# Block-product order, a sixth lead slab, and the state-space preparation of a hybrid retention / S5 decoder

## The chip, the cores and the metric

The kernel runs on one core of a Trainium2 chip. The metric is the device time of one execution in microseconds; the median of three runs before the change is 2788.43 us (2788.19 to 2794.11). The engines that matter here are PE (TensorE, the matrix multiplier), DVE (VectorE), ACT (ScalarE), POOL (GpSimd) and SP (SyncE, which issues most loads). Each engine runs its own list of instructions in the order in which the program wrote them, and waits on semaphores of the others. Matrix products accumulate in the banks of PSUM, 128 x 512 float32 numbers each.

## The reference

One sequence of 1024 tokens, width 1024, two layers: a retention mixer, then a state-space (S5) mixer. Each mixer is followed by a conv-gated MLP of inner width 2816, each sub-layer is normalised and shifted by a condition vector, and a final norm follows. What the change touches is the MLP's first half, and the tables of the S5 layer that depend on parameters alone:

```python
def conv_ffn(h, w_up, conv_w, conv_b, w_down):
    val, gate = jnp.split(h @ w_up, 2, axis=-1)
    gate = lax.conv_general_dilated(gate, conv_w, ...) + conv_b   # depthwise, causal, width 3
    return (jax.nn.silu(gate) * val) @ w_down

# s5_mixer: powers of exp((lam_re + i*lam_im)*dt) per group and state, hence cos and sin of many angles
for i in range(2):
    ...
    x = x + g1 * (retention_mixer(h, ...) if i % 2 == 0 else s5_mixer(h, ...))
    h = rms_norm(x) * (1.0 + sc2) + sh2
    x = x + g2 * conv_ffn(h, ...)
```

## The kernel before, in words

**One pair.** The 2816 columns of gate and val are cut into 22 slabs of 128. One slab of both is a *pair*. Its 2 x 2 block product (two halves of the tokens, two halves of the width) is not made with eight block products but with seven, named A11, S2, S3, S1, A22, A12, S4, and sums on both sides. Each is 4 slices x 3 matmuls of 128 x 512, since float32 operands are split into a high and a low part (`mm3`, L765 to L767, three lines for the three terms). So a pair is 84 matmuls.

**Banks and readers.** A11 goes to bank b1; ACT copies it to `u`, and A12 is later added into b1. S2 goes to b2, and DVE adds it to `u`. S3 goes to b4; DVE reads it (`g1 = u + b4`, L1210, in the profile `E<-tu,bk`), and A22 is then added into the same b4, which DVE reads again (`E<-tu,bk` a second time). S1 goes to b3, is read by DVE (`E<-E,bk`), and S4 is added into b3. A22 therefore waits for the `g1` addition: A22 overwrites what `g1` still has to read. After A22 come the convolution (`conv_start` on ACT, `conv_mid` L1638 and L1639 on DVE four times, `conv_end` on ACT) and two products by DVE.

**What feeds it.** The weights arrive in quarters. POOL makes sums of quarters (L128, `sq`, `wr`), and every one of the seven weight operands is split into high (L334, ACT) and low (L335, DVE) parts, two DVE instructions ahead in the schedule. `W.get` names the operand a product wants, and the order of the splits follows the order of the products (`Q7`).

**Lead slabs.** The MLP starts while the second half of the tokens is still being normalised. `lead()` computes A11 and A12 of the first `LEADS` slabs (24 matmuls each), which need the first half alone, keeping the results in SBUF tiles `uv`; the first `LEADS` pairs then run the five products `Q5` (S2, S3, S1, A22, S4). Meanwhile `Norm.steps_s`, a generator moved on by `nrm.step`, makes the sums of normalised halves (tiles `ht`, `hl`, `hg`) and their high and low parts (`hs`): the high by ACT, the low by DVE or POOL.

**Background work.** During the first MLP the S5 tables are made by `s5_weights`, a generator that `bg(steps)` moves on after each product of a pair, and by two after the last one. A `yield True` ends a call of `bg` at once. One block of eight (`j`) has two halves; each does outer products on POOL (L128, `ar<-sp`), transposes through bank 6 (L1392), five DVE instructions on angles (L1396 twice, L1398, L798, L1400; the tile `sev`), two Sin on ACT (L1402, L1403), a second outer product on POOL (9 columns), and matmuls into bank 7 (L1414).

## Time and profile before

| | |
|---|---|
| median of three runs | 2788.43 us |
| profiled execution, its own time | 2790.11 us |
| span of the profile | 2788.3 us |
| PE busy | 2628.9 us (94%), 12777 instructions |
| DVE busy | 1763.3 us (63%) |
| POOL busy | 1055.6 us (38%) |
| ACT busy | 932.5 us (33%) |
| chain that ended last | PE 64%, DVE 18%, ACT 6%, issue 4%, DMA 4%, POOL 2% |

The first MLP's up-projection runs from about 917 to 1445 us of the span (lead products, pairs 0 to 4 with five products, pairs 5 to 21 with seven), the second one's from about 2069 to 2521 us. In the views, "busy" is the time in which an engine executed; "idle before" is the time it stood still ahead of an instruction, with what ended that. PEclk is the clock that was granted to PE as a share of 2.4 GHz; at 0.5 it is 1.2 GHz. The kernel's own line numbers stand in the rows.

### The profile page before, as it was taken

Reading aid. Unit: us, or ns where it says so; the run is one execution under the profiler, and the core shown is the slowest. Engines: PE = TensorE matmul, PEld = TensorE weight load, DVE = VectorE, ACT = ScalarE, POOL = GpSimd, SP = SyncE. Lnnn points to the kernel's source line nnn. Section 1 sums busy time; section 2 is a strip of 40 time slices with the busy share of each in tenths; the row PEclk is TensorE's granted clock in tenths of the full one; section 3 lists DMA queues with packets and bytes.
Section 4 is the critical chain, followed back from the end, with each engine's and each line's share of the span. In section 5 each row is a group of like instructions: output and inputs, shape, how many; then the busy total and the mean of one; then the engine's idle time right before and its main releaser. Section 6 shows DMA issues by size and latency. Waiting matters only on the chain.

```text
span 2788.3 us, 33464 instructions
## 1 busy us (share of the span) xinstructions
PE 2628.9 (94%) x12777; PEld 2199.2 (79%) x12777; DVE 1763.3 (63%) x2347; ACT 932.5 (33%) x1486; POOL 1055.6 (38%) x817
## 2 busy tenths in 40 slices
PE   6999999999999888999989999999998999999998
PEld 5798888888888676777777877888876788888887
DVE  8664664746765787777776654674248876666454
ACT  5332131221322634444433323322144444343112
POOL 5455676765101544655523333221124422310004
PEclk7999999999999999999999999999999999999999
DMA  7644344343532223333345433795221322225211
GB/s 241 169 129 137 121 135 145 117 158 94 168 115 69 91 93 106 119 108 119 113 176 183 137 127 129 248 301 184 75 83 61 106 83 84 83 86 207 101 53 61
DMA packets 319756, 356.59 MB, mean 128 GB/s; under 512 B 39372, under 2 KB 261100, under 8 KB 319596
## 3 DMA queue, kind: packets, MB, share of 16 engines
q1 hardware_dynamic: 278316, 276.17, 31.7%
q10 hardware_dynamic: 41280, 78.28, 7.6%
q8 instruction: 101, 1.65, 0.2%
q14 instruction: 59, 0.48, 0.1%
HBM read 266.64 MB, written 86.15 MB: 127 GB/s over the span
## 4 chain that ended last, share of the span: by engine, by line
PE 64%; DVE 18%; ACT 6%; issue 4%; DMA 4%; POOL 2%; SPq 0%; ACTq 0%; DVEq 0%; POOLq 0%
PE bk L765 20%; PE bk L767 19%; PE bk L766 19%; DVE t L1639 1%; DVE t L1638 1%; DVE whi L335 1%; DVE E L1210 1%; DVE wlo L335 1%; PE bk L1077 1%; PE bk L1075 1%; PE bk L1076 1%; DVE t L1210 1%; DVE sev L1396 1%; POOL ar L128 1%; DMA U<-u_d 1%
## 5 line engine op out<-in xcount | busy, mean ns | idle before, releaser
L765 PE MATMUL bk<-hs,whi 128*128 128x512 f32 x656 | 268.4, 409 | 44.7 <-DVE E L1210 41.2
L1473 DVE SCALAR_TENSOR_TENSOR x<-bk,mods,x 128x512 f32<-128x512 f32 x224 | 184.6, 832 | 192.5 <-PE bk L767 192.4
L766 PE MATMUL bk<-hs,whi 128*128 128x512 f32 x656 | 265.5, 405 | 6.4 <-DVE hs L657 4.3
L322 DVE TENSOR_TENSOR wlo<-wr,whi 128x1024 fp32r<-128x1024 f32 x126 | 179.7, 1430 | 138.4 <-ACT whi L321 138.4
L765 PE MATMUL bk<-hh,whi 128*128 128x512 f32 x640 | 255.7, 400 | 8.3 <-DVE x L1473 4.1
L767 PE MATMUL bk<-hs,wlo 128*128 128x512 f32 x656 | 260.2, 397 | 0.0
L766 PE MATMUL bk<-hl,whi 128*128 128x512 f32 x640 | 253.4, 396 | 3.0 <-POOL hl L128 1.7
L765 PE MATMUL bk<-hs,wlo 128*128 128x512 f32 x576 | 229.4, 398 | 26.0 <-DVE E L1210 26.0
L767 PE MATMUL bk<-hh,wlo 128*128 128x512 f32 x640 | 252.4, 394 | 0.2 <-DVE wlo L322 0.2
L767 PE MATMUL bk<-hs,whi 128*128 128x512 f32 x576 | 231.0, 401 | 0.0
L766 PE MATMUL bk<-hs,wlo 128*128 128x512 f32 x576 | 227.1, 394 | 0.0
L321 ACT ACTIVATE whi<-wr 128x1024 fp32r<-128x1024 f32 x126 | 131.5, 1056 | 284.6 <-PE bk L766 226.1
L765 PEld LDWEIGHTS bk<-hs,whi 128*128 128x128 f32 x656 | 128.7, 196 | 78.2 <-issue 28.1
L765 PE MATMUL bk<-fh,whi 128*128 128x512 f32 (+1 forms) x480 | 183.2, 382 | 5.3 <-ACT nat L2229 3.7
L767 PE MATMUL bk<-fh,wlo 128*128 128x512 f32 (+1 forms) x480 | 181.0, 377 | 0.0
L766 PE MATMUL bk<-fl,whi 128*128 128x512 f32 (+1 forms) x480 | 180.8, 377 | 0.0
L457 POOL TENSOR_TENSOR aacc<-aacc,ar 128x1024 f32<-128x1024 f32 x70 | 172.4, 2463 | 5.8
L128 POOL TENSOR_TENSOR nacc<-nacc,ar 128x512 f32<-128x512 f32 x36 | 46.6, 1294 | 322.1 <-ACT ar L575 321.9
L766 PEld LDWEIGHTS bk<-hs,whi 128*128 128x128 f32 x656 | 129.4, 197 | 34.8 <-DVE hs L657 5.0
L765 PEld LDWEIGHTS bk<-hs,wlo 128*128 128x128 f32 x576 | 110.2, 191 | 53.9 <-ACT wlo L334 12.5
L765 PEld LDWEIGHTS bk<-hh,whi 128*128 128x128 f32 x640 | 122.3, 191 | 35.4 <-ACT hh L611 4.5
L128 POOL TENSOR_TENSOR ar<-sp 128x512 f32<-128x512 f32 (+1 forms) x64 | 83.2, 1314 | 175.8 <-ACT sev L1402 81.8
(375 smaller groups left out, 6706.1 us busy)
## 6 DMA issues: line engine op xcount, KB each, us to landing
ar<-in_ada_w SPq DMA_DIRECT2D x80, 512.0 KB, 4.4
wr<-in_ffn_w_up SPq DMA_DIRECT2D x74, 512.0 KB, 3.8
wr<-in_ret_w_in SPq DMA_DIRECT2D x48, 512.0 KB, 3.8
ff_d<-t ACTq DMA_DIRECT2D x44, 512.0 KB, 2.8
wr<-in_ffn_w_down SPq DMA_DIRECT2D x44, 512.0 KB, 4.2
fr<-ff_d SPq DMA_DIRECT2D x44, 512.0 KB, 5.8
x_d<-x ACTq DMA_DIRECT2D x24, 512.0 KB, 3.1
x<-x_d SPq DMA_DIRECT2D x24, 512.0 KB, 7.2
```

Source lines behind the costliest of these rows:

```text
L128: GP.tensor_tensor(out=out, in0=in0, in1=in1, op=op)
L321: A.activation(out=hi, in_=r, func=AF.Copy)
L322: low = lambda: V.tensor_tensor(out=lo, in0=r, in1=f(hi), op=ALU.subtract)
L335: V.tensor_tensor(out=lo, in0=src, in1=f(hi), op=ALU.subtract)
L457: eng.tensor_tensor(out=acc, in0=acc, in1=raw, op=ALU.add)
L765: PE.matmul(bk, lhsT=lh, rhs=rh, start=first, stop=False, skip_group_check=skip)
L766: PE.matmul(bk, lhsT=lh, rhs=rl, start=False, stop=False, skip_group_check=skip)
L767: PE.matmul(bk, lhsT=ll, rhs=rh, start=False, stop=last, skip_group_check=skip)
L1075: PE.matmul(o, lhsT=hh, rhs=wh[:, k % 4, :], start=(k == 0), stop=False)
L1076: PE.matmul(o, lhsT=hh, rhs=wl[:, k % 4, :], start=False, stop=False)
L1210: V.tensor_tensor(out=o, in0=a, in1=b, op=op)
L1473: V.scalar_tensor_tensor(out=dst, in0=bk, scalar=g, in1=src, op0=ALU.mult, op1=ALU.add)
```

## The change

It has four parts.

1. `Q7` has A12 ahead of A22, so that there are two products (S1, A12) between S3 and A22 in bank b4. The multiplication by b1 stays behind `conv_end`. `next_(5)` moves with A12.
2. `LEADS` is 6. `lead()` handles three slabs, then three; the val results of the last three stay in their PSUM banks until their pair has used them (`vv += bks`), so that the last two copies by ACT (L1759) go, and the lead pairs 0 to 2 rotate over three banks (2, 3, 4).
3. In `steps_s` six of the subtractions that make a low part per MLP go from POOL to DVE: two for t1, two for t3, two for t4.
4. In `s5_weights` the rounded angle `kq` lies in the `sev` tile and no longer in `tb`; the transposed outer product is copied out in two pieces (384 and 128 columns) into free ends of `tb` and `ta`, with two DMAs; `outer(9)` comes right behind the transposes and no longer behind Sin; each step ends its call of `bg`, and a pair moves the generator on once after each of six products and not at all after the seventh (before: eight).

The diff:

```diff
-    LEADS = 5
+    LEADS = 6
-    Q7 = ("A11", "S2", "S3", "S1", "A22", "A12", "S4")
+    Q7 = ("A11", "S2", "S3", "S1", "A12", "A22", "S4")
...
+    def hard(n):
+        for _ in range(n):
+            yield True
...
-                    parts(t1, S.t1, pool=True)
+                    parts(t1, S.t1, pool=i % 2 == 0)
...
-                parts(low[i], S.t3, pool=i % 2 == 1, then=partial(S.lh.put, low[i]))
+                parts(low[i], S.t3, then=partial(S.lh.put, low[i]))
...
-                parts(t2[i], S.t4, pool=i % 2 == 1, then=gone)
+                parts(t2[i], S.t4, then=gone)
...
-        kq = tb[:, HW:T]
+        kq = ev0
...
-                yield True
-                yield True
-                yield True
+                yield from hard(3)
                 bk = bank(6)
                 for g in range(4):
                     PE.transpose(bk[:, g * P:(g + 1) * P], ta[:, g * P:(g + 1) * P], ident)
-                A.activation(out=ev0, in_=bk, func=AF.Copy)
-                A.dma_start(out=p1_d[j, :, cs4], in_=ev0)
+                A.activation(out=tb[:, 640:T], in_=bk[:, 0:384], func=AF.Copy)
+                A.activation(out=ta[:, 896:T], in_=bk[:, 384:HW], func=AF.Copy)
+                A.dma_start(out=p1_d[j, :, hf * HW:hf * HW + 384], in_=tb[:, 640:T])
+                A.dma_start(out=p1_d[j, :, hf * HW + 384:(hf + 1) * HW], in_=ta[:, 896:T])
+                outer(9, O_AR, O_AI, O_Q1, O_Q2, False)
                 for c_ in (TWO_PI_1, TWO_PI_2):
                     V.scalar_tensor_tensor(out=ev1, in0=kq, scalar=-c_, in1=ev1, op0=ALU.mult, op1=ALU.add)
-                yield
+                yield True
                 V.scalar_tensor_tensor(out=ev1, in0=kq, scalar=-TWO_PI_3, in1=ev1, op0=ALU.mult, op1=ALU.add)
                 clamp_angle(ev1)
                 V.scalar_tensor_tensor(out=kq, in0=ev1, scalar=-1.0, in1=ev1, op0=ALU.mult, op1=ALU.max)
-                yield
+                yield True
...
-                yield
-                outer(9, O_AR, O_AI, O_Q1, O_Q2, False)
-                yield True
-                yield True
                 yield True
...
-                bg(steps * (2 if i == 6 else 1))
+                bg(steps if i < 6 else 0)
...
+            if val0 is None:
+                product(b1, q("A12"), SB.b1[4:8], False)
+                next_(5)
+                after(5)
             product(b4, q("A22"), SB.t4, False)
...
-            if val0 is None:
-                product(b1, q("A12"), SB.b1[4:8], False)
-                next_(5)
             tt(ts[:, 0, :], ts[:, 0, :], b1 if val0 is None else val0, ALU.mult)
...
-            uu = [tu[:, 0, :], tu[:, 1, :], halves[2], halves[4], halves[6]]
-            vv = [halves[0], halves[1], halves[3], halves[5], halves[7]]
+            uu = [tu[:, 0, :], tu[:, 1, :]] + halves[3:7]
+            vv = halves[0:3]
...
-            ws = [W.get(("uv", l, 3)), W.get(("uv", l, 4), more=True)]
+            ws = [W.get(("uv", l, i), more=(i > 3)) for i in range(3, LEADS)]
...
-            for i, bk in enumerate(bks):
-                A.activation(out=vv[3 + i], in_=bk, func=AF.Copy)
-                free_bank(bk)
-            W.done(2)
+            vv += bks
+            W.done(3)
...
-            else:
+            elif ff != 3:
                 drop(keep.pop(0))
+            if ff > 2:
+                free_bank(vv[ff])
```

**The order, place 1.** DVE in the first MLP, from behind the convolution of pair 15 to the `g1` addition of pair 16. `tu` is `u`, `bk` a bank; `whi` and `wlo` are the splits; `sev` are the angle steps; `E<-tu,bk` at the end is `g1`. Before (its `g1` comes two rows later, behind one more split):

```order
L335 TENSOR_TENSOR wlo<-wr,wlo 128x512
L1210 TENSOR_TENSOR t_7742<-t_7742,bk 128x512
L1210 TENSOR_TENSOR tu<-tu,bk 128x512
L1210 TENSOR_TENSOR t_7742<-t_7742,tu 128x512
L335 TENSOR_TENSOR whi<-sq,whi 128x512
L335 TENSOR_TENSOR wlo<-wrx,wlo 128x512
L1396 SCALAR_TENSOR_TENSOR sev<-ar,sev 128x512 x2
L335 TENSOR_TENSOR whi<-sq,whi 128x512
L1398 SCALAR_TENSOR_TENSOR sev<-ar,sev 128x512
L798 TENSOR_SCALAR sev<-sev 128x512
L1400 SCALAR_TENSOR_TENSOR ar<-sev 128x512
L1210 TENSOR_TENSOR tu<-tu,bk 128x512
```

After:

```order
L1214 TENSOR_TENSOR t_7742<-t_7742,bk 128x512
L1214 TENSOR_TENSOR tu<-tu,bk 128x512
L1214 TENSOR_TENSOR t_7742<-t_7742,tu 128x512
L335 TENSOR_TENSOR whi<-sq,whi 128x512
L335 TENSOR_TENSOR wlo<-wr,wlo 128x512
L335 TENSOR_TENSOR whi<-sq,whi 128x512
L1214 TENSOR_TENSOR tu<-tu,bk 128x512
L335 TENSOR_TENSOR wlo<-wrx,wlo 128x512
L1401 SCALAR_TENSOR_TENSOR sev<-sev 128x512 x2
L1214 TENSOR_TENSOR E<-tu,bk 128x8x64
L335 TENSOR_TENSOR whi<-wr,whi 128x512
L1403 SCALAR_TENSOR_TENSOR sev<-sev 128x512
```

Between the convolution's end and `g1`, five splits and all five angle steps lay before; now it is four splits and the first two angle steps, and the other three follow `g1`.

**Place 2.** DVE in the second MLP, pair 0, from the addition of S2 to `u` up to `g1`. `ht<-hf,ht` makes the difference of halves t4, `hs<-ht,hs` its low part. Before:

```order
L1210 TENSOR_TENSOR tu<-tu,bk 128x512
L706 TENSOR_TENSOR ht<-hf,ht 128x512 x2
L657 TENSOR_TENSOR hs<-ht,hs 128x512
L706 TENSOR_TENSOR ht<-hf,ht 128x512 x2
L657 TENSOR_TENSOR hs<-ht,hs 128x512
L1210 TENSOR_TENSOR E<-tu,bk 128x8x64
```

After:

```order
L1214 TENSOR_TENSOR tu<-tu,bk 128x512
L710 TENSOR_TENSOR ht<-hf,ht 128x512 x2
L661 TENSOR_TENSOR hs<-ht,hs 128x512
L710 TENSOR_TENSOR ht<-hf,ht 128x512
L661 TENSOR_TENSOR hs<-ht,hs 128x512
L710 TENSOR_TENSOR ht<-hf,ht 128x512
L661 TENSOR_TENSOR hs<-ht,hs 128x512 x2
L1214 TENSOR_TENSOR E<-tu,bk 128x8x64
```

Two more `hs<-ht,hs` stand ahead of `g1`.

**Place 3.** POOL at the same time. `hs<-...` are low parts (`ar` t1, `hl` t3, `ht` t4, `hg` the fourth set), the rest sums of weight quarters. Before:

```order
L128 TENSOR_TENSOR hs<-ar,hs 128x512 x4
L128 TENSOR_TENSOR hs<-hl,hs 128x512 x2
L128 TENSOR_TENSOR aacc<-wr 128x512
L128 TENSOR_TENSOR aacc<-aacc,wra 128x512
L128 TENSOR_TENSOR wr<-wra,wr 128x512
L128 TENSOR_TENSOR wra<-wra,aacc 128x512
L128 TENSOR_TENSOR hs<-ht,hs 128x512 x2
L128 TENSOR_TENSOR hs<-hg,hs 128x512 x2
```

After:

```order
L128 TENSOR_TENSOR hs<-ar,hs 128x512 x2
L128 TENSOR_TENSOR aacc<-wr 128x512
L128 TENSOR_TENSOR aacc<-aacc,wr 128x512
L128 TENSOR_TENSOR wr<-wr 128x512
L128 TENSOR_TENSOR wr<-wr,aacc 128x512
L128 TENSOR_TENSOR aacc<-wra 128x512
L128 TENSOR_TENSOR aacc<-aacc,wr 128x512
L128 TENSOR_TENSOR wra<-wr,wra 128x512
L128 TENSOR_TENSOR wr<-wr,aacc 128x512
L128 TENSOR_TENSOR hs<-hg,hs 128x512 x2
```

Six `hs` are gone (two of `ar`, two of `hl`, two of `ht`), and the sums of weights follow earlier.

## Rows read from the trace of the kernel before

**Rows 1.** Work by stretch: length, busy (count) per engine, PEclk, DMA share, GB/s

```profile
1072.60:1105.70 33.10, 23.28 (x96) 18.19 (x95) 25.42 (x29) 12.99 (x24) 16.31 (x13) 0.85 0.30 97
1105.70:1423.80 318.10, 291.29 (x1261) 234.95 (x1260) 240.82 (x288) 141.79 (x243) 170.90 (x138) 0.96 0.35 114
...
2216.50:2502.10 285.60, 285.60 (x1261) 236.56 (x1260) 195.07 (x271) 118.02 (x213) 79.80 (x57) 1.00 0.26 85
```

**Rows 2.** PE's waits, whole run: line <- releaser: us, times, longest

```profile
PE bk L765 <- DVE E L1210: 67.2, 21, 9.8
...
PE bk L1414 <- POOL ar L128: 12.5, 6, 3.1
...
PE bk L765 <- ACT uv L1751: 2.4, 2, 1.2
```

**Rows 3.** PE's waits, 1105.7 to 1423.8 (first MLP, pairs 7 to 20)

```profile
PE bk L765 <- DVE E L1210: 22.8, 7, 5.1
```

**Rows 4.** PE's waits, 1072.6 to 1105.7 (first MLP, pair 6)

```profile
PE bk L765 <- DVE E L1210: 9.8, 1, 9.8
```

**Rows 5.** PE's waits, 2106.4 to 2216.5 (second MLP, pairs 0 to 5)

```profile
PE bk L765 <- DVE E L1210: 16.2, 5, 5.9
```

**Rows 6.** VectorE's waits, 1105.7 to 1423.8

```profile
DVE wlo L335 <- ACT wlo L334: 29.6, 19, 3.3
...
DVE E L1210 <- PE bk L767: 7.7, 8, 1.9
```

**Rows 7.** VectorE's groups, 1105.7 to 1423.8: busy us, mean ns, idle before

```profile
L1638 DVE SCALAR_TENSOR_TENSOR t<-E,prm,t 128x512 f32<-128x512 f32 x28 | 29.7, 1062 | 10.7 <-ACT E L1628 10.7
...
L1396 DVE SCALAR_TENSOR_TENSOR sev<-ar,sev 128x512 f32<-128x512 f32 x14 | 19.3, 1376 | 0.8 <-POOL ar L1386 0.5
```

**Rows 8.** The same view, second MLP, 2216.5 to 2502.1

```profile
L1638 DVE SCALAR_TENSOR_TENSOR t<-E,prm,t 128x512 f32<-128x512 f32 x30 | 22.5, 749 | 5.7 <-ACT E L1628 5.7
```

**Rows 9.** VectorE in time, from pair 19 to pair 20: start, us, instruction

```profile
1390.82 0.68 DVE L1210 TENSOR_TENSOR E<-tu,bk 128x512 f32<-128x512 f32 x1
...
1398.68 0.69 DVE L335 TENSOR_TENSOR wlo<-wr,wlo 128x512 fp32r<-128x512 f32 x1 [1.31 <-ACT wlo L334]
...
1399.89 3.11 DVE L1396 SCALAR_TENSOR_TENSOR sev<-ar,sev 128x512 f32<-128x512 f32 x2
...
1404.22 0.69 DVE L1400 SCALAR_TENSOR_TENSOR ar<-sev 128x512 f32<-128x512 f32 x1
...
1411.41 0.67 DVE L1210 TENSOR_TENSOR E<-tu,bk 128x512 f32<-128x512 f32 x1
```

**Rows 10.** VectorE in time, from pair 5 to pair 6

```profile
1070.52 0.67 DVE L1210 TENSOR_TENSOR E<-tu,bk 128x512 f32<-128x512 f32 x1
...
1081.14 3.40 DVE L1396 SCALAR_TENSOR_TENSOR sev<-ar,sev 128x512 f32<-128x512 f32 x2
...
1092.81 0.67 DVE L1210 TENSOR_TENSOR E<-tu,bk 128x512 f32<-128x512 f32 x1
```

**Rows 11.** PE in time around pair 6's wait (start, us, instruction)

```profile
1093.63 0.77 PE L765 MATMUL bk<-hs,whi 128*128 128x512 f32 x1 [9.82 <-DVE E L1210]
1094.19 0.63 PE L766 MATMUL bk<-hs,whi 128*128 128x512 f32 x1
```

**Rows 12.** VectorE in time, second MLP's pairs 0 and 1

```profile
2111.37 2.88 DVE L706 TENSOR_TENSOR ht<-hf,ht 128x512 f32<-128x512 f32 x2
2114.18 1.76 DVE L657 TENSOR_TENSOR hs<-ht,hs 128x512 fp32r<-128x512 f32 x1
2115.86 3.42 DVE L706 TENSOR_TENSOR ht<-hf,ht 128x512 f32<-128x512 f32 x2
...
2119.81 0.68 DVE L1210 TENSOR_TENSOR E<-tu,bk 128x512 f32<-128x512 f32 x1
...
2136.53 0.69 DVE L1210 TENSOR_TENSOR t<-t,uv 128x512 f32<-128x512 f32 x1 [0.79 <-ACT t L1642]
```

**Rows 13.** What POOL waits for, whole run

```profile
POOL ar L128 <- ACT sev L1402: 81.8, 16, 12.2
```

More of the change, by code (lines that the diff above doesn't have):

```diff
@@ L1432, in s5_weights @@
                              in_=ks_d[j * 8:(j + 1) * 8, :, P - GI * t:2 * P - GI * t].rearrange("g i w -> i g w"))
-            yield True
-            yield True
-            yield True
-            yield True
-            yield True
-            yield True
+            yield from hard(6)
             A.activation(out=tb.rearrange("p (g j t) -> p g t j", g=8, t=8),
@@ L1441, in s5_weights @@
             A.dma_start(out=t_d[j], in_=tb)
-            yield True
-            yield True
+            yield from hard(2)
         drop(sev)
@@ L1702, in pair @@
                 free_bank(b1)
-                after(5)
             product(b3, q("S4"), SB.b2, False)
@@ L1751, in lead @@
                         A.activation(out=uu[3 + i], in_=bk, func=AF.Copy)
-                    if kh and i == 0:
+                    if kh and i == 1:
                         if not nrm.marked:
```

## The prediction, made before the changed kernel ran

> **What bounds the kernel now.** I read the work by stretch first, then what PE waits for, then VectorE's own waits, then VectorE in time at three places. PE is busy for 94% of the span, so a gain must be time in which PE stands still or runs at the lower of its two clocks. The second MLP's steady stretch shows what an undisturbed pair costs: 285.60 us for 15 pairs of 84 matmuls, PE busy throughout, clock 1.00 [rows 1]. So a pair is 285.60/15 = 19.04 us, a product 2.72 us, a matmul 0.2267 us. The first MLP's pairs 7 to 20 take 318.10 us at a clock of 0.96, although 14 undisturbed pairs are 266.6 us. Part of the rest is the state-space matmuls, the rest is waiting and clock.
>
> PE's largest wait, 67.2 us in 21 places, is for VectorE's addition into E (L1210) [rows 2]: a second product into bank b4 (A22) waits until `g1` has read S3's. Pairs 7 to 20 hold 22.8 us of it in 7 waits [rows 3], pair 6 alone 9.8 us in one [rows 4], the second MLP's lead pairs 16.2 us [rows 5]. Is VectorE late because it waits for PE, or because it has too much to do? In pairs 7 to 20 it waits ahead of an E addition for PE only 7.7 us in all, and 29.6 us for ACT's high halves of weights [rows 6]. So it is VectorE's own list that is late. Part of its length is stretching: a convolution step takes 1062 ns there [rows 7] against 749 ns in the second MLP [rows 8], where no state-space work runs beside it. An angle step takes 1376 ns [rows 7].
>
> The loop to look at runs from VectorE's second E addition of one pair (after A22) to `g1` of the next and to that pair's A22. PE does six products in it, 6 x 2.72 = 16.3 us. At pair 20 VectorE needs from 1390.82 to 1411.41 + 0.67, that is 21.3 us [rows 9]; the excess is PE's wait. A12 ahead of A22 by itself leaves this loop at six products; what it moves is how VectorE's work is shared. It puts 5.4 us of PE work behind S3, not 2.7 us, so that `g1` may come 2.7 us later, and the loop's next stretch loses as much.
>
> **The change part by part.** All sums are against the profiled execution of 2790.11 us; the median is 1.68 us lower, and I subtract that at the end.
>
> First MLP, pairs 7 to 20. With the new order one split of a weight leaves the stretch between the convolution and `g1`. At pair 20 that split is 0.69 us, with a wait of 1.31 us ahead of it [rows 9]. The convolution's end has to wait for the silu in its place, which costs about 0.8 us by the 0.79 us of idle time that a lead pair, without such a split, shows there [rows 12]; net 1.2 us for each of the 7 waits, 8.4 us. Second, the angle steps: counted in the two orders, 32 of the 45 that fall into the pairs lie in this loop's stretch from E to `g1` before, and 25 after, the others between `g1` and the second E, where PE now has three products (8.2 us) to hide them and had two. Five of them at pair 20 take from 1399.89 to 1404.91, 5.0 us or 1.0 us each [rows 9]. Of the 7 moved, 7/9 are in this stretch (7 of 9 half-blocks): 5.4 us. Together 13.8 of the 22.8 us; bounds 0 (VectorE is as late as before) and 22.8.
>
> With the waits some of the clock comes back: after pair 6's wait the next matmul stands with 0.63 us [rows 11], and 0.96 of 318.1 us leaves 12.7 us lost in the stretch [rows 1]. I take 5 us, a bit less than the share of the waits that goes (bounds 0 and 12.7).
>
> First MLP, pairs 0 to 6. The sixth lead slab gives PE 24 matmuls, 5.4 us, while VectorE still normalises: its lateness at pair 0 shrinks by as much. Pair 6's wait: from E at 1070.52 to `g1` at 1092.81 VectorE does all five angle steps, the first two in 3.40 us [rows 10]. In the new order the steps stand just behind `g1` of pair 6. I take 8 of the 9.8 us and 2.5 us of clock (0.85 over 33.1 us lost 5.0 [rows 1]). Against that: the steps before them now lie ahead of `g1` of pair 5, and pair 5 now has five products; 5 us by pair 20's steps, from 0 to 7. The lead pairs rotate over three banks, so S1 of a pair waits until VectorE has read S4's sum of the pair before: 2 us, from 0 to 5 x 0.68 = 3.4, if VectorE is on time. The moved subtractions: VectorE gets six in each MLP, POOL loses them. A subtraction took 0.68 to 1.76 us, and a difference of halves beside POOL 2.88/2 to 3.42/2 us [rows 12]. Two of the six stand ahead of pair 0's `g1`; the other four fall into the lead products' time, where the extra 5.4 us cover 4 x 0.68. So 1.4 us, from -3 (POOL no longer stretches the differences to 1.7 us) to 10.6 (six at 1.76, uncovered). Net for this stretch: -5.4 - 8 - 2.5 + 5 + 2 + 1.4 = -7.5.
>
> POOL's waits. The second outer product no longer stands behind the Sin, for which POOL waits 81.8 us in 16 places [rows 13]. PE's matmuls L1414 wait for that product 12.5 us in 6 places [rows 2]. I take 10 us (bounds 0 and 12.5). The extra copy and DMA on ACT cost nothing I can see: ACT is busy for 141.79 of 318.10 us [rows 1]; uncovered, 9 of them at the 0.68 us of an addition of that size [rows 9] would be 6.
>
> Second MLP. The sixth slab gives 5.4 us against the 16.2 us of waits [rows 5], the banks take 2, and the subtractions about nothing, since VectorE's stretch from 2111.37 to 2119.81 is half stretching already [rows 12]: -3.4. Of the waits for ACT's last copies of val, 2.4 us [rows 2], half goes: -1.2.
>
> Sum: -13.8 - 5 - 7.5 - 10 - 3.4 - 1.2 = -40.9. 2790.1 - 40.9 = 2749.2, less 1.7: **2747.5 us**.
>
> **The rivals.** *All of these waits go* (chance 0.12). VectorE has slack enough: in the second MLP it is busy for 195.07 of 285.60 us and PE never waits [rows 1]. Then 67.2 + 12.5 us of waits and 12.7 us of clock in pairs 7 to 20 go, less 7 for pair 5 and the banks: -85.4, 2703 us. Against it: in the first MLP VectorE is busy for 240.82 of 318.10 us, and 67 us of the remaining 77 would have to be usable.
>
> *VectorE stays the bound* (0.18). Steps that leave one half of the loop make the other half late: then the first MLP gains only POOL's 10 us and the second its 4.6: 2790.1 - 14.6 - 1.7 = 2774 us. For it: VectorE waits for PE only 7.7 us [rows 6].
>
> *It does not do what it says* (0.09). POOL's waits turn into waits for E at the same pairs, and the lead slab is used up by pair 5 and the subtractions: 2788 us, within a few us.
>
> *Slower by collision* (0.16). The second outer product is now issued in the same breath as the angle steps, so POOL works in SBUF while VectorE makes all five of them. Before, POOL waited for Sin and worked later. Then each step goes to the 1.7 us that the slowest pair of them shows (3.40/2 [rows 10]): two of them from the mean of 1.376 [rows 7], three from 0.69 at best (the last at pair 20 [rows 9]), 0.65 + 3.0 = 3.65 us for each of 9 half-blocks, 32.9 us. Less the 14.6 above: +18.3, 2807 us. It decides once VectorE's list in a loop grows by more than what the new order takes from it (13.8 us in the 14 pairs); for it speaks that almost nothing on VectorE there waits for PE [rows 6].
>
> The convolution steps show the stretching: 1062 against 749 ns [rows 7, 8]. The Trainium skill, "SBUF — State Buffer", section "Who interferes with whom", says of it that VectorE and GpSimd share one pair of ports under an exclusive lock, so that a VectorE instruction which needs that second pair (two SBUF inputs) and a GpSimd instruction keep each other out. The trace agrees: the E additions, which take one input from PSUM, kept 0.67 to 0.68 us beside it [rows 9, 10]. By the rule alone the collision rival would be the likeliest, with 2807 us. I leave it at 0.16: of pair 20's five steps the first two took 3.11 us and the last 0.69 [rows 9], so a run of steps is not stretched throughout.
>
> **How the numbers follow.** The forecast has 0.45; its own range is 2725 to 2770, from the bounds of the terms taken together. A measurement of this kernel can tell about 0.2%, 5.6 us, from no change. Faster than that are the forecast, the full gain and VectorE as the bound: 0.45 + 0.12 + 0.18 = 0.75; the same 0.09; slower 0.16. The range leaves out the collision (0.16) and little else: from 2700, just under the full gain, to 2790, just over no change.
>
> **What would show each step.** Right: PE's wait for E (L1210) falls from 67.2 to 40 us or less, pair 6's 9.8 us wait is gone, L1414's waits fall below 4 us, the stretch of pairs 7 to 20 takes about 295 us at a clock of 0.97 or more, and a new small wait stands at S1 in lead pairs. Wrong: the waits for E keep their sum and stand elsewhere (VectorE is the bound); L1396's mean rises from 1376 to 1600 ns or more (collision); the lead pairs' waits rise, so the moved subtractions were dearer than the cover of the sixth slab.

## The result

The changed kernel takes 2818.24 us (median of four runs, 2816.87 to 2819.31); the kernel before, run beside it, 2790.06 us. The ratio is 1.0099, 95% interval 1.0081 to 1.0116: **1% slower, 28 us, where 41 us of gain were forecast**. The time lies above the stated range, 28 us beyond its upper end of 2790.

Work by stretch, the changed kernel (columns as in [rows 1]). The stretches are: first MLP's lead products, pairs 0 to 5, pair 6, pairs 7 to 20, pair 21 with the down projection; second MLP's lead products, pairs 0 to 5, pairs 6 to 20:

```profile
921.10:969.40 48.30, 40.16 (x160) 31.14 (x161) 36.69 (x45) 30.16 (x49) 22.71 (x17) 0.89 0.23 73
969.40:1078.40 109.00, 89.93 (x374) 71.76 (x373) 85.03 (x108) 42.12 (x78) 47.30 (x36) 0.92 0.29 91
1078.40:1101.90 23.50, 21.76 (x90) 17.18 (x89) 22.50 (x22) 8.64 (x17) 17.23 (x13) 0.93 0.26 79
1101.90:1427.60 325.70, 293.90 (x1270) 235.17 (x1269) 249.60 (x292) 146.72 (x258) 175.99 (x141) 0.95 0.35 114
1427.60:1735.60 308.00, 281.54 (x1242) 227.00 (x1241) 181.22 (x203) 100.55 (x129) 106.00 (x93) 0.97 0.43 147
2090.30:2141.60 51.30, 40.71 (x161) 31.65 (x160) 36.18 (x45) 28.97 (x48) 21.21 (x16) 0.90 0.17 52
2141.60:2247.70 106.10, 91.89 (x361) 73.65 (x360) 82.80 (x107) 40.41 (x75) 37.74 (x25) 0.90 0.25 80
2247.70:2533.30 285.60, 285.60 (x1261) 236.56 (x1260) 195.58 (x273) 117.26 (x212) 86.09 (x59) 1.00 0.28 89
```

The same view of the kernel before, for the stretches that do not stand in [rows 1]:

```profile
918.20:955.80 37.60, 33.09 (x136) 26.29 (x137) 28.32 (x42) 28.35 (x46) 18.28 (x16) 0.91 0.20 65
1423.80:1715.50 291.70, 278.77 (x1242) 226.13 (x1241) 171.58 (x200) 98.56 (x119) 97.18 (x92) 0.98 0.44 153
2067.00:2106.40 39.40, 33.44 (x137) 26.10 (x137) 27.98 (x42) 27.30 (x45) 17.01 (x15) 0.91 0.13 41
```

Lead products and pairs 0 to 6 of the first MLP gained: from 187.5 to 180.8 us (pair 6 from 33.1 to 23.5). Pairs 7 to 20 lost 7.6 us (318.1 to 325.7), the stretch of pair 21 and the down projection **16.3 us** (291.7 to 308.0, with the same 1242 matmuls), the second MLP's lead products and pairs 0 to 6 **7.9 us** (168.6 to 176.5; pair 6 is 19.04 in the changed kernel). The steady second MLP is 285.6 us in both.

What PE waits for over the whole run, changed kernel (answers to [rows 2]; L769 is the old L765, L1394 the old L1392, L1415 the old L1414):

```profile
PE bk L769 <- DVE E L1214: 36.1, 16, 7.5
...
PE bk L1394 <- POOL ar L128: 11.4, 4, 5.0
PE bk L769 <- DVE tu L1214: 10.7, 3, 5.1
...
PE bk L769 <- ACT sev L1407: 8.6, 1, 8.6
PE bk L769 <- DVE uv L1214: 7.6, 4, 2.4
...
PE bk L769 <- ACT tu L1659: 6.5, 3, 3.7
...
PE bk L1415 <- POOL ar L128: 1.8, 2, 1.2
```

Read it against [rows 2]: the wait for E fell from 67.2 to 36.1 us and the one at the state-space matmuls from 12.5 to 1.8, both as forecast. That is 41.8 us less. But four waits came up (10.7 + 8.6 + 7.6 + 6.5), and the transposes L1394 wait for POOL for 11.4 us (4.0 before): together 40.8 us more. Over the whole span PE stands still for 179.8 us (159.4 before), and its same 12777 instructions keep it busy for 7.6 us more.

### The profile page after: what moved, and what is told of

It reads as the page before. It is cut to its first block, busy times and chain, and to the rows that moved or that the text cites. A ratio compares the mean times of both kernels' runs of the same rounds, so it can differ in the third digit from the quotient of the medians.

```text
span 2816.3 us, 33497 instructions
## 1 busy us (share of the span) xinstructions
PE 2636.5 (94%) x12777; PEld 2201.5 (78%) x12777; DVE 1780.8 (63%) x2357; ACT 931.5 (33%) x1496; POOL 1051.4 (37%) x805
## 4 chain that ended last, share of the span: by engine, by line
PE 59%; DVE 16%; issue 8%; ACT 6%; POOL 5%; DMA 4%; SPq 1%; ACTq 1%; POOLq 0%; DVEq 0%
PE bk L769 18%; PE bk L771 18%; PE bk L770 18%; POOL ar L128 3%; DVE t L1634 2%; DVE t L1633 1%; DVE wlo L335 1%; DVE E L1214 1%; PE bk L1081 1%; PE bk L1079 1%; PE bk L1080 1%; DVE whi L335 1%; DVE hs L661 1%; DMA fr<-ff_d 1%; SPq L1432 1%
## 5 line engine op out<-in xcount | busy, mean ns | idle before, releaser
L769 PE MATMUL bk<-hs,whi 128*128 128x512 f32 x664 | 268.7, 405 | 33.9 <-DVE E L1214 13.0
L769 PE MATMUL bk<-hs,wlo 128*128 128x512 f32 x568 | 231.9, 408 | 44.4 <-DVE E L1214 23.2
L771 PE MATMUL bk<-hs,wlo 128*128 128x512 f32 x664 | 269.4, 406 | 2.4 <-DVE wlo L322 2.4
L769 PE MATMUL bk<-hh,whi 128*128 128x512 f32 x640 | 255.3, 399 | 9.4 <-DVE x L1468 5.9
L770 PE MATMUL bk<-hs,wlo 128*128 128x512 f32 x568 | 228.8, 403 | 0.0
L769 PE MATMUL bk<-fh,whi 128*128 128x512 f32 (+1 forms) x480 | 183.1, 381 | 3.7 <-ACT nat L2224 3.1
L769 PEld LDWEIGHTS bk<-hs,whi 128*128 128x128 f32 x664 | 128.9, 194 | 68.3 <-issue 13.9
L128 POOL TENSOR_TENSOR nacc<-nacc,ar 128x512 f32<-128x512 f32 x36 | 46.6, 1294 | 335.7 <-ACT ar L579 335.6
L769 PEld LDWEIGHTS bk<-hs,wlo 128*128 128x128 f32 x568 | 111.2, 196 | 74.6 <-DVE E L1214 22.1
L771 PEld LDWEIGHTS bk<-hs,wlo 128*128 128x128 f32 x664 | 131.2, 198 | 31.8 <-DVE wlo L322 3.3
L769 PEld LDWEIGHTS bk<-hh,whi 128*128 128x128 f32 x640 | 122.4, 191 | 36.3 <-ACT hh L615 6.3
```

The costliest lines, as they stand in the source:

```text
L128: GP.tensor_tensor(out=out, in0=in0, in1=in1, op=op)
L769: PE.matmul(bk, lhsT=lh, rhs=rh, start=first, stop=False, skip_group_check=skip)
L770: PE.matmul(bk, lhsT=lh, rhs=rl, start=False, stop=False, skip_group_check=skip)
L771: PE.matmul(bk, lhsT=ll, rhs=rh, start=False, stop=last, skip_group_check=skip)
```

## The experiments

Each kernel was timed beside the kernel before. The columns of this table are the medians' difference to that (us), the ratio's 95% interval, and from each profile four stretches: first MLP from its lead products to the end of pair 6; pairs 7 to 20; pair 21 and down projection; second MLP from its lead products to the end of pair 6.

| kernel | difference | ratio, interval | 0 to 6 | 7 to 20 | 21, down | second, 0 to 6 |
|---|---|---|---|---|---|---|
| before | | | 187.5 | 318.1 | 291.7 | 168.6 |
| changed | +28.2 | 1.0081 to 1.0116 | 180.8 | 325.7 | 308.0 | 176.5 |
| a_only | -4.8 | 0.9972 to 0.9994 | 179.7 | 313.6 | 294.2 | 167.0 |
| l_only | +15.1 | 1.0037 to 1.0073 | 189.2 | 317.6 | 297.6 | 175.1 |
| s_only | +29.2 | 1.0083 to 1.0126 | 192.6 | 331.7 | 304.8 | 168.3 |
| no_s | +10.4 | 1.0025 to 1.0046 | 187.2 | 312.9 | 299.9 | 173.9 |
| p_only | +2.6 | 0.9999 to 1.0021 | 186.9 | 318.9 | 292.2 | 172.3 |
| s_gap | +37.5 | 1.0124 to 1.0154 | 182.5 | 320.5 | 328.6 | 170.2 |
| s_fix | -3.6 | 0.9979 to 0.9998 | 188.4 | 318.6 | 285.7 | 169.0 |
| b3 | +2.7 | 1.0001 to 1.0022 | 186.4 | 317.8 | 290.1 | 173.0 |
| l4 | +12.3 | 1.0034 to 1.0064 | 189.5 | 317.4 | 298.0 | 176.0 |
| l_t4 | +14.4 | 1.0030 to 1.0069 | 188.8 | 317.7 | 297.4 | 176.0 |
| lead4 | +11.5 | 1.0028 to 1.0057 | 184.5 | 317.1 | 300.3 | 172.9 |
| a_sfix | -4.9 | 0.9976 to 0.9994 | 178.8 | 314.7 | 291.6 | 168.4 |
| l_sfix | -4.8 | 0.9972 to 0.9991 | 181.4 | 325.2 | 282.3 | 175.4 |
| after_sfix | **-11.9** | 0.9944 to 0.9974 | 176.4 | 317.4 | 286.5 | 172.9 |
| after_tb | +17.6 | 1.0053 to 1.0087 | 181.2 | 324.5 | 299.5 | 173.7 |
| aps_fix | -5.5 | 0.9966 to 0.9989 | 180.8 | 314.2 | 291.4 | 168.5 |

### The parts one by one

The diffs of a_only, l_only, s_only and p_only are the parts 1, 2, 4 and 3 of the change; no_s is parts 1 to 3.

> The kernel before with A12 ahead of A22 alone (Q7 and the place of the product and its step). Theory 1 (the order is a gain, as forecast: one split and some angle steps leave the loop): about 14 us faster, PE's wait for E at A22 falls from 67 us to about 50. Theory 2 (VectorE's list stays the bound, the loop is six products either way): 0 +- 5 us, and the waits for E keep their sum. Theory 3 (the order brings its own wait: A12 now follows A11's copy by three products, not four, and S4 follows A22's reader): 5 to 10 us slower, with PE waiting for ACT's copy of u at A12.

The order is a gain, smaller than theory 1 has it: 4.8 us, with the wait for E at 52.0 us (forecast about 50). It brings the wait of theory 3 too, but a short one: at pair 6 the 9.8 us of [rows 4] become 3.6 us, now at A12. PE's waits with the order alone, first in pair 6, then for E in pairs 7 to 20, where they were 22.8 us [rows 3]:

```profile
PE bk L765 <- ACT tu L1664: 3.6, 1, 3.6
...
PE bk L765 <- DVE E L1210: 14.1, 7, 3.6
```

> The kernel before with six lead slabs alone, three of them kept in PSUM, and the three-bank rotation that follows. Theory 1 (the extra slab covers VectorE, as forecast: 5.4 us in each MLP against 2 for the banks): 5 to 10 us faster. Theory 2 (the rotation over three banks makes S1 of each lead pair wait for VectorE's reading of S4's sum of the pair before, which stands late in VectorE's list; in the changed kernel these waits are 9.4 us in the first MLP and 9.8 us in the second): about 10 us slower over both MLPs, and most of the 7.9 us that the second MLP's lead stage grew by in the changed kernel shows here.

15 us slower, more than either theory says. The second MLP's share of it, 6.5 us, is there as theory 2 has it; how it comes about is tested below.

> The kernel before with the state-space part alone (angle buffer, early second outer product, even steps). Theory 1 (POOL's waits go, as forecast): about 10 us faster, waits at the matmuls L1414 fall from 12.5 us to about 2. Theory 2 (what the early outer product takes from one wait it gives to the next: the transposes wait for POOL instead, and in the down projection each step of the generator now ends its call, so the work falls on other places): about 16 us slower, nearly all of it between the first MLP's last pair and the end of its down projection, where the changed kernel lost 11 to 16 us.

Nearer to theory 2, but 13 us worse: the part alone costs as much as the whole change. And the loss is not where theory 2 puts it: more than half of it lies in the pairs (5.1 and 13.6 us), the rest in the down projection (13.1 us).

> The changed kernel without its state-space part (order, lead slabs and moved subtractions stay). If the state-space part makes the loss (theory 2 of that run): about 16 us faster than the changed kernel, so 10 to 13 us slower than before. If the loss is the lead slabs' banks and the order: still 25 to 28 us slower than before. If the parts only cost together: near the time of before.

The first of the three: 10.4 us slower than before, so 18 us of the 28 go with the state-space part.

> The moved subtractions alone (six in each MLP from POOL to VectorE). Forecast: about 1.4 us slower in the first MLP and nothing in the second. By the three parts measured so far (order -5, lead slabs +15, and +10 for these three together) it should be 0 +- 3 us. Rival (VectorE is the bound in the lead stage, so six more of its instructions at 0.68 to 1.76 us in each MLP show in full): 8 to 15 us slower.

Six more subtractions for VectorE in each MLP cost 2.6 us, which this cannot tell from nothing (the interval holds 1); the rival falls.

### What the state-space part does wrong

The last two half-blocks, in time. First the kernel before, PE's state-space matmuls and VectorE's first two angle steps (start, us, instruction, idle before and what ended it):

```profile
1621.25 0.89 PE L1392 MATMUL bk<-cst,ar 128*128 128x128 f32 x4 [3.33 <-POOL ar L128]
1632.58 1.05 PE L1414 MATMUL bk<-ar,sp 128*16 128x128 f32 x8 [0.86 <-POOL ar L128]
1639.82 0.60 PE L1392 MATMUL bk<-cst,ar 128*128 128x128 f32 x4
```

```profile
1624.63 2.43 DVE L1396 SCALAR_TENSOR_TENSOR sev<-ar,sev 128x512 f32<-128x512 f32 x2 [1.69 <-POOL ar L1386]
```

Then the changed kernel: PE, VectorE, ACT and POOL at that place.

```profile
1625.94 0.66 PE L1394 MATMUL bk<-cst,ar 128*128 128x128 f32 x4 [1.47 <-POOL ar L128]
1633.98 1.05 PE L1415 MATMUL bk<-ar,sp 128*16 128x128 f32 x8 [1.22 <-POOL ar L128]
1646.37 1.11 PE L1394 MATMUL bk<-cst,ar 128*128 128x128 f32 x4 [5.00 <-POOL ar L128]
```

```profile
1629.32 3.35 DVE L1401 SCALAR_TENSOR_TENSOR sev<-sev 128x512 f32<-128x512 f32 x2 [1.03 <-POOL sev L1390]
...
1633.25 1.22 DVE L1403 SCALAR_TENSOR_TENSOR sev<-sev 128x512 f32<-128x512 f32 x1
```

```profile
1635.70 0.72 ACT L1407 ACTIVATE sev<-sev,cst 128x512 f32<-128x512 f32 x1 [6.00 <-DVE sev L1405]
...
1638.60 1.19 ACT L1417 ACTIVATE sev<-ar 128x512 f32<-128x512 f32 x1 [1.56 <-DMA cs_d<-sev]
...
1640.19 0.38 ACT L1422 ACTIVATE ar<-bk 16x256 f32<-16x256 f32 x1 [0.40 <-ACT sev L1417]
```

```profile
1640.64 0.24 POOL L128 TENSOR_TENSOR ar<-ar,db 16x32 f32<-16x32 f32 x1 [6.72 <-ACT ar L1422]
...
1641.95 2.17 POOL L128 TENSOR_TENSOR ar<-sp 128x512 f32<-128x512 f32 x2
```

From the bottom up: the next transposes wait for POOL's outer product, which stands in POOL's list behind the small addition L128; that waits for ACT's copy L1422; that stands behind the permuted copy L1417, which waits for the stores of cos and sin; and all of it stands in ACT's list behind Sin, which waits 6.00 us for VectorE's last angle step. The early outer product has left this circle, but Sin has not: PE had the matmuls done at 1635, and their result is fetched at 1640. A round takes 20.4 us (1625.94 to 1646.37) where it took 18.6, and all of the difference lies ahead of Sin, which comes 9.8 us after the transposes (7.8 before, Sin at 1629.00); from Sin to the next transposes it is 10.7 us, and was 10.8. Two things make Sin late here. The first two angle steps, now beside POOL's early outer product, take 3.35 us (2.43 before) and the third 1.22 (0.69 before). And each step ends its call of `bg`, so that an addition of the down projection, 0.74 us, has come between the second step and the third.

So POOL's wait for Sin, 81.8 us in [rows 13], did not go. It stands some instructions later now, at ACT's copy, and with the wait that was already there the sum is nearly the same: 81.8 + 68.4 = 150.2 us before, 150.7 now. POOL's wait for this copy in the kernel before, and then in the changed kernel:

```profile
POOL ar L128 <- ACT ar L1421: 68.4, 29, 9.6
```

```profile
POOL ar L128 <- ACT ar L1422: 150.7, 31, 13.1
```

Three kernels test this.

s_gap: part 4 alone, and behind Sin's stores

```diff
-                yield True
+                yield from hard(3)
```

> The state-space part alone, with two more steps between Sin and the matmuls L1414 (three steps lie between them, as between the early outer product and the matmuls before). Theory (the loss of this part is that Sin, the stores of cos and sin, and the copy into the same tile now stand one step ahead of the matmuls' evacuation, so ACT waits for the stores, POOL for ACT and the next transposes for POOL): ACT's wait for the stores, 19.9 us in 10 places in the run of that part alone, falls below 5 us, POOL's 178 us of waiting for ACT's copy L1422 shrinks, and 15 us or more of the 29 us come back. Rival (the early outer product itself collides with the angle steps): the 29 us stay.

The wait for the stores falls to 4.4 us as expected, and against the part alone the pairs come back (10.1 us in 0 to 6, 11.2 in 7 to 20). Yet the kernel is slower, because the generator has more steps and is not through when the last group of the down projection begins: what is left is then issued at once (`bg_drain`). ACT waits there for a load of that work, and the split that PE needs stands behind it in ACT's list. PE's waits from pair 21 to the end of the down projection in s_gap:

```profile
PE bk L1394 <- POOL ar L128: 17.4, 4, 9.5
PE bk L769 <- ACT whi L321: 14.4, 1, 14.4
PE bk L1415 <- POOL ar L128: 10.7, 2, 5.9
```

s_fix: part 4 alone, matmuls and evacuation ahead of Sin, the permuted copy in `tb`

```diff
-                A.activation(out=ev0, in_=kq, func=AF.Sin, ...)   # and the second Sin, both stores
-                yield True
                 w9 = ta[:, 0:576].rearrange("p (g w) -> p g w", g=4)
...
-                A.activation(out=ev0.rearrange(...), in_=w9[...], func=AF.Copy)
-                A.dma_start(out=w1_d[j, :, cs4], in_=ev0)
+                A.activation(out=tb[:, 0:HW].rearrange(...), in_=w9[...], func=AF.Copy)
+                A.dma_start(out=w1_d[j, :, cs4], in_=tb[:, 0:HW])
...
+                yield True
+                A.activation(out=ev0, in_=kq, func=AF.Sin, ...)   # and the second Sin, both stores
                 yield
```

> The state-space part alone, with the matmuls L1414, their evacuation and POOL's additions ahead of Sin, and the permuted copy put into a free part of the tile tb, so that nothing in the chain from the second outer product to the next first one waits for Sin or its stores. Theory: ACT's wait for the stores is gone, PE's waits at the transposes (15.9 us) fall below 6 us, and the run is 20 us or more faster than the state-space part alone, near or below the time of before. Rival (collision of the early outer product with the angle steps): as slow as the state-space part alone.

33 us better than the part alone, and 3.6 us faster than before. POOL's wait for the copy (L1417 here), and the last rounds on PE:

```profile
POOL ar L128 <- ACT ar L1417: 45.6, 30, 8.3
```

```profile
1609.11 0.60 PE L1394 MATMUL bk<-cst,ar 128*128 128x128 f32 x4
1614.54 1.05 PE L1410 MATMUL bk<-ar,sp 128*16 128x128 f32 x8 [0.72 <-POOL ar L128]
1623.82 0.60 PE L1394 MATMUL bk<-cst,ar 128*128 128x128 f32 x4
```

This round is 14.7 us, and the transposes in it do not wait (3.4 us in the whole run, 15.9 with the part alone). The early outer product is still beside the angle steps and still stretches them, but Sin is no longer in the round. So the longer steps by themselves do not cost the time; they count where Sin stands ahead of the evacuation.

after_tb: the changed kernel with the second edit of s_fix only, the permuted copy in `tb`

> The changed kernel with one of the two edits of the mend: the permuted copy goes into tb and no longer into the tile whose cos and sin are being stored; the matmuls stay behind Sin. Theory 1 (ACT's wait for the stores, 13.5 us in 9 places, is what holds up the evacuation, POOL and the next transposes): 25 us or more of the 38 us that the whole mend brought. Theory 2 (it is the place behind Sin: the evacuation waits on ACT for VectorE's angle steps, 66.2 us in 14 places): less than 12 us come back.

Theory 2: by the differences to the kernel before (+28.2, +17.6, and -11.9 for the whole mend, below) the stores are 10.6 of 40.1 us; the rest comes only when the evacuation stands ahead of Sin. Here too POOL waits 129.0 us for the copy, and ACT 65.2 us for the angle steps.

### What the lead slabs do

b3: five slabs, three banks held idle during the lead pairs 

```diff
+            spare = [new_bank() for _ in range(3)]
...
+            if ff == LEADS - 1:
+                for t_ in spare:
+                    free_bank(t_)
...
```

> The kernel before with five lead slabs, where the lead pairs may use three banks of PSUM only (three more are held idle and given back behind pair 4). Theory (the loss of the lead part is the three-bank rotation): 8 to 15 us slower than before, with waits of PE for VectorE's tu and uv at S1 as in the lead part alone (21.8 us there). Rival (the loss is the sixth lead pair itself, with its five products and less cover): within 3 us of before.

The rival. The waits at S1 are there, 12.7 us for tu and uv in the second MLP, but they replace most of those at A22. PE's waits in the second MLP's pairs 0 to 5, b3:

```profile
PE bk L765 <- DVE uv L1210: 7.2, 3, 2.7
PE bk L765 <- DVE E L1210: 5.9, 1, 5.9
PE bk L765 <- DVE tu L1210: 5.5, 2, 5.3
```

That is 18.6 us against 16.2 [rows 5]. The banks cost 2.7 us in all, not 15, although the second MLP's stretch alone grew by 4.4 us.

l4: six slabs, four val results copied to SBUF

```diff
-            uu = [tu[:, 0, :], tu[:, 1, :]] + halves[3:7]
-            vv = halves[0:3]
+            uu = [tu[:, 0, :], tu[:, 1, :]] + halves[4:8]
+            vv = halves[0:4]
...
-            vv += bks
+            A.activation(out=vv[3], in_=bks[0], func=AF.Copy)
+            free_bank(bks[0])
+            vv += bks[1:]
...
```

> Six lead slabs, with four val results copied out to SBUF and two kept in PSUM, so that the lead pairs rotate over four banks; then no product of a lead pair waits for S4's reader. Theory (bank rotation): the lead part's 15 us go, within 5 us of before or a few us faster by the sixth slab's cover. Rival (the sixth lead pair itself): 10 to 15 us slower, as with three banks.

The rival: the sixth slab itself.

l_t4: six slabs, with one step of the normalisation behind the lead products

```diff
         keep, uu, vv = lead()
...
+        nrm.step(1)
```

> The lead part alone (six slabs), with one more step of the normalisation taken behind the lead products, so that VectorE makes the difference t4 ahead of pair 0 and not between pair 0's S2 and g1. Theory (the sixth slab's 5.4 us are lost because VectorE stands idle in them, for instance 3.4 us ahead of the addition of S2 to u, while t4's work stays behind S2): 4 us or more in each MLP come back, so 8 us or more against the lead part alone (15 us slower than before). Rival (the loss is the three banks, or the sixth pair's shorter run of products, whatever VectorE does in the lead stage): still 12 to 18 us slower than before.

That theory falls as well. In the second MLP the wait at pair 1 falls from 5.3 to 1.3 us, but the one at pair 0 grows from 2.5 to 7.3.

lead4: four slabs, one of them in the second group

```diff
-    LEADS = 5
+    LEADS = 4
...
-            ws = [W.get(("uv", l, 3)), W.get(("uv", l, 4), more=True)]
+            ws = [W.get(("uv", l, 3))]
...
```

> The kernel before with four lead slabs, not five. Theory (a lead slab takes 24 matmuls, 5.4 us, out of pairs in which VectorE is late, and puts them where VectorE has nothing to do with the time): the other way round it gains, 3 to 10 us faster over both MLPs. Rival (the lead products do cover VectorE's normalisation): 8 to 12 us slower, with longer waits for E at pairs 0 and 1.

Slower too, so five is the best of the three with the old state-space part. But not for the rival's reason: in the second MLP's pairs 0 to 6 PE waits for E 9.0 us (16.2 with five slabs [rows 5]), and the first MLP's lead products and pairs 0 to 6 take 3.0 us less. The loss stands in the second MLP's lead stage (4.3 us) and in the stretch from pair 21 on (8.6).

Where the sixth slab's time goes in the second MLP, where no state-space work runs: its 24 matmuls are 5.4 us, but the lead products take 10.3 us longer (39.4 to 49.7 in l_only). PE's waits in the second MLP's lead products, l_only:

```profile
PE bk L765 <- ACT uv L1751: 2.7, 1, 2.7
...
PE bk L767 <- DVE wlo L322: 1.2, 1, 1.2
```

In the kernel before the first is 1.2 us (half of the 2.4 in [rows 2]) and the second is not there. In all PE stands still for 9.4 us in these lead products, 6.0 before, and is busy for 6.9 us more. Pairs 0 to 6 of the second MLP give back only 3.8 us (129.2 to 125.4 in l_only), because each five-product pair waits for VectorE again. In l4 the waits for E sum to 16.1 us in six places, against 16.2 in five [rows 5]: the lateness is spread over one pair more, and its sum stays. PE's waits in the second MLP's pairs 0 to 6, l4:

```profile
PE bk L765 <- DVE E L1210: 16.1, 6, 4.7
```

### Whether the parts hinder each other

All four have the edit of s_fix: a_sfix is parts 1 and 4, l_sfix parts 2 and 4, after_sfix the whole change, aps_fix the whole change without part 2.

> The order part together with the state-space part as mended (matmuls and their evacuation ahead of Sin, permuted copy in tb), five lead slabs, subtractions where they were. If the two gains add: 4.8 + 3.6, about 8 us faster than before. If both work on the same late loop of VectorE: no more than 5 us faster.

The second: 4.9 us, no more than the order alone.

> Six lead slabs together with the mended state-space part. In the lead part alone the lead stages and pairs 0 to 6 of both MLPs lost 8 us together, and the stretch from pair 21 to the end of the first down projection another 6 us. Theory (that second loss is the state-space chain, which a lead pair moves on by six steps and not eight, so that it meets the down projection at another point): with the mended chain, which waits less, the down stretch is back at 286 to 290 us and the run is about 5 us slower than before (8 for the lead stages less 3.6 for the mended chain). Rival (the loss behind the pairs has to do with the lead slabs in another way): 10 us or more slower.

4.8 us *faster* than before. The down projection is at 282.3 us where l_only had 297.6, so the lead part's loss behind the pairs goes with the state-space chain, as that theory said; the pairs 0 to 6 of the first MLP gained too (189.2 to 181.4), and pairs 7 to 20 lost 7.6.

> The changed kernel with nothing but its state-space part mended (matmuls and evacuation ahead of Sin, permuted copy in tb). If the loss of 28 us is the sum that the single parts gave (about 17 us for the state-space part on top of the other three, the rest the lead slabs): 17 to 25 us faster than the changed kernel, 3 to 11 us slower than before. If something else in the combination makes the loss: less than 10 us come back.

More than the single parts gave: 38 us back by medians, **2780.28 us, the fastest of all, 0.9959 of before (0.9944 to 0.9974)**. POOL waits 74.8 us for the copy here.

> The changed kernel with the mended state-space part, but with five lead slabs as before. In the second MLP six slabs cost about 4 us net in every profile with them. If the sixth slab still costs when the chain is mended: faster than the changed kernel with the mend alone (2780 us), by 3 to 8 us. If the sixth slab gains once the chain does not stand in its way: 3 to 8 us slower than that.

2786.04 us: with the mended chain the sixth slab is worth about 5 us by the ratios (0.9978 and 0.9959, whose intervals overlap), although the second MLP's lead stage is 4.4 us longer with it (168.5 to 172.9).

## Why the prediction was wrong

**The step that failed is "POOL's waits" (-10 us).** It took the wait of L1414 out and asked only where the second outer product stands, not what stands behind Sin in ACT's list. The wait at L1414 did go (12.5 to 1.8 us), but the round from one transpose to the next has Sin, the stores and the evacuation in it, and grew by 1.8 us where it was tightest. The forecast counted the extra copy and DMA on ACT against ACT's busy share, 141.79 of 318.10 us; a share says nothing about one chain. The price: part 4 alone is +29.2 us, mended -3.6. By stretch, the sum is off most in pairs 7 to 20 (-18.8 forecast, +7.6 measured), then in pair 21 with the down projection (+16.3, where the forecast had no loss) and in the second MLP's lead stage.

**The sixth slab (-5.4 + 2 in each MLP).** "Its lateness at pair 0 shrinks by as much" is true of pair 0: in the second MLP its wait fell from 5.9 us to 2.7 in l4. The step failed in taking that for the end: the lead products grew by twice their matmuls' time, and the later pairs waited as before. Forecast -3.4 for the second MLP's lead stage, measured +7.9 in the changed kernel. The bank term was about right in price (2 us forecast in each MLP, 2.7 us for both in b3).

**Pairs 0 to 6 of the first MLP (-7.5)** came to -6.7, with pair 6 from 33.1 to 23.5 us (9.6 less, 10.5 forecast). Pair 6 was foreseen; that the sum fits is luck, since the order alone gave -7.8 here, while the lead part alone gave +1.7 and the state-space part alone +5.1.

**Pairs 7 to 20 (-13.8 - 5)**: the order alone gave -4.5 (318.1 to 313.6). The mechanism holds there (the wait for E falls from 22.8 to 14.1 us), the size does not: the 1.2 us for each split was measured nowhere but at pair 20. In the changed kernel nothing of it is left. PE waits for E as long as before, 22.8 us, and for ACT's copy of `u` at A12 another 6.5 us, which was not in the sum. The forecast's own sign for this was "the waits for E keep their sum". PE's wait for E in this stretch in no_s, in the changed kernel and in after_sfix:

```profile
PE bk L765 <- DVE E L1210: 8.7, 7, 4.0
```

```profile
PE bk L769 <- DVE E L1214: 22.8, 10, 7.5
```

```profile
PE bk L769 <- DVE E L1214: 22.6, 8, 5.1
```

So beside the state-space part, mended or not, the order's gain here is small. Some of this is an exchange, as one of the rivals below had it: without that part PE waits 11.1 us at L1414 in this stretch, with it 0.6. The waits for E, at L1414 and at the transposes together are 26.8 us before, 19.8 in no_s and 25.3 in the changed kernel. What makes up the rest, no run here shows. The wait at L1414 in no_s:

```profile
PE bk L1414 <- POOL ar L128: 11.1, 2, 6.6
```

One reading behind this term was wrong as well. The prediction set 29.6 us of waiting for ACT's high halves [rows 6] against 7.7 for PE, and concluded that VectorE's own list is late. The same view has a second such row, so that VectorE waits for ACT for 54.5 of the 77.3 us in which it stands still. In the changed kernel it is 47.3 us, but VectorE is busy for 249.6 us, not 240.8. The row left out, then both rows of the changed kernel:

```profile
DVE whi L335 <- ACT whi L334: 24.9, 18, 2.5
```

```profile
DVE whi L335 <- ACT whi L334: 33.5, 15, 4.5
DVE wlo L335 <- ACT wlo L334: 13.8, 10, 1.7
```

**The rivals.** Collision was priced at 2807 us, 11 us from the result, but by a sum that did not come about: in pairs 7 to 20, where it set its 33 us, the first two angle steps became shorter (1376 ns in [rows 7]). In the down projection, which it did not look at, they did become longer. The changed kernel in pairs 7 to 20; then pair 21 with the down projection before, in the changed kernel and in s_fix:

```profile
L1401 DVE SCALAR_TENSOR_TENSOR sev<-sev 128x512 f32<-128x512 f32 x14 | 18.0, 1285 | 0.2
```

```profile
L1396 DVE SCALAR_TENSOR_TENSOR sev<-ar,sev 128x512 f32<-128x512 f32 x14 | 14.5, 1034 | 3.6 <-POOL ar L1386 3.4
```

```profile
L1401 DVE SCALAR_TENSOR_TENSOR sev<-sev 128x512 f32<-128x512 f32 x14 | 21.8, 1556 | 9.5 <-POOL sev L1390 9.2
```

```profile
L1401 DVE SCALAR_TENSOR_TENSOR sev<-sev 128x512 f32<-128x512 f32 x14 | 20.5, 1463 | 2.9 <-POOL sev L1390 2.6
```

The steps are stretched beside POOL's product, so the rule of the Trainium skill ("SBUF — State Buffer", section "Who interferes with whom") is not contradicted. It was not what decided, as s_fix shows: its steps are stretched almost as much, and it is faster than before.

The rival by which POOL's waits turn into waits for E at the same pairs was the nearest in mechanism, at 0.09. It was held to end within a few us; the waits went not to E alone but to the transposes, to A12 and to the down projection, for which the forecast has no term of its own, although 7 of the 16 half-blocks run there.

**What stays open.** The effects of the parts do not add: the lead part costs 15 us with the old chain, and with the mended one and the other parts the sixth slab gains about 5. What is shown is that the stretch from pair 21 on moves by 15 us (297.6 to 282.3) with the state-space part alone. Why the order gains less in pairs 7 to 20 beside part 4 even when that is mended, why four slabs lose 8.6 us from pair 21 on, and which step of the generator must meet which product, was not settled.

## What to carry to other kernels

When an operation is taken out of a chain, follow the whole round back to itself through each engine's list, and see which other member still stands there. A wait that turns up again with much the same sum (150.2 and 150.7 us) is a hint that it has only changed its name; it is no measure, since this sum was 74.8 us in after_sfix and 101.7 in a_sfix, and both are faster than before. An operation that nobody in the round needs (Sin here) belongs behind the round's evacuation on its engine, not ahead of it. And do the parts of such a change one by one: here one part cost 29 us alone, and with it mended the whole gained 12.

## What the runs showed that was not expected

- Work in the background has a deadline: with two steps more per half-block (s_gap) the pairs recovered 21 us, and with the drain at its end the down projection's stretch took 24 us more than with the part alone.
- A second product into a bank that waits for a reader costs little more with fewer banks free: most of the wait moves from A22 to S1 (18.6 against 16.2 us in the second MLP).
- The sum of PE's waits does not tell what they cost in clock: in pairs 0 to 5 of the second MLP PE stood still for 14.2 us in the changed kernel and ran at a granted clock of 0.90, between its two levels of 2.4 and 1.2 GHz; in the kernel before it stood still for 16.2 us and ran at 0.94.
